# Which engine computes the rounding rest of h, of the first weight pieces and of the first half of h2

## The chip, the cores and the metric

One core of one Trainium2 chip runs the whole program. The metric is the time of one execution on the device in microseconds (us): 1650.13 us as the median of 3 runs (1648.28 to 1652.7) before the change. About 0.3% (5 us) is what a measurement of this kernel can tell from no change.

## The reference, cut to what matters

One decoder layer, batch 1, 1024 rows (positions) by 1024 columns, all in float32:

```
[shift1, scale1, gate1, shift2, scale2, gate2] = SiLU(c) W_ada + b_ada
h  = LN(x) * (1 + scale1) + shift1
one projection h W_in -> GLA q,k,v,r,gate | SWA q,k,v | branch gates
y  = sigmoid(g_A) * GLA + sigmoid(g_B) * SWA
x  = LN_1(alpha * x + gate1 * (y W_o))
h2 = LN(x) * (1 + scale2) + shift2
u  = causal conv3(h2 W_up);  f = GELU(u_gate) * u_val
x  = LN_2(alpha * x + gate2 * (f W_down))
```

The kernel multiplies with more precision than one matmul of rounded operands has: it writes each operand as a rounded part (`hi`, in the type float32r) and the rest and sums three matmuls: hi by hi, hi by lo, lo by hi. So each operand tile of 128 x 512 costs a rounding copy and a subtraction on some engine before TensorE can use it. The change is about which engine does that for three groups of tiles.

## The kernel before, in words

The order of TensorE's instructions is written by hand: the functions are called in TensorE's order, and pieces that hang on other engines (transposes, attention, layer norms) are put into a queue with `at(delay, cost, fn)` and called once a count of TensorE's expected time (`now`) has passed their due time. The other engines' instructions are ordered by the framework's planner, which works with its own costs; each engine then works through its own list in order, and an instruction that waits holds up those behind it on that engine. All loads go through SyncE's queue (SP), in order; `wst` (a weight piece as loaded, 256 KB) has 4 buffers, `aw` (a piece of W_ada) 4 in the first stage, `raw` 6 in the last.

**The head (0 to about 80 us).** x is normalised tile by tile (`norm_x`: two `bn_stats` and a `bn_aggr` on VectorE, three tiny operations on GpSimd, L361, L362 and L378, and the scaling on ScalarE, L480). The shift and scale of h come in 8 groups of 128 columns (`c` = 0 to 7): group 0 on TensorE, groups 1 to 7 as chains of 8 operations on VectorE (`mod1_part`, L525 and L527, each reading a piece `aw`), closed by a matmul with ones on TensorE (L537) and an addition on VectorE (`mods`, L538). For each group and each half of the rows `h_part` calls `to_half`: 4 transposes on TensorE (L388), the scaling into `ss` on ScalarE (L392), the rounding into `hi` on ScalarE (L397), the rest into `lo` on GpSimd (L398). TensorE multiplies it with the first weights right away (`kv_mm`, 5 PSUM banks at once, L338 to L340). These are 16 calls of `to_half`.

**The weight stream.** `ws.emit_to(n)` loads weight pieces ahead (L246), rounds on ScalarE (L253), and computes the rest (L254): on GpSimd for the first 8 pieces, which are those of the head, on VectorE for the other 100.

**Around h2 (about 900 to 1010 us).** The last output-projection units (`o_unit`, L338 to L340, evacuated on VectorE by L983) are followed per row tile by `ln_a` (layer norm with affine: statistics, GpSimd's L361 and L362, then L1068 and L1069 on VectorE) and `ln_b` (a second norm: statistics, GpSimd's three operations, L1074 on ScalarE). After row tile 3 the first half of h2 is made (`h2_part(0, kt)`, 8 calls): 4 transposes (L1085), scaling on ScalarE (L1090) into a buffer `xt` of the tag `raw`, rounding on VectorE (L1093), rest on GpSimd (L1094). After row tile 7 the second half follows (`h2_part(1, kt)`, with differences of the two halves, L1076, for a product by a Strassen-like scheme). In the same stretch the first pieces of W_up are combined on GpSimd (L1213 to L1219), the first of the 17 first products run on TensorE (L1268 to L1270), and gate2 is summed on VectorE (L602).

`split_to` (L381) is the helper that rounds on ScalarE and subtracts on VectorE; the rest of the kernel already uses it for h2's second half and for W_up and W_down.

Of the kernel before, what the change touches and what calls it, by code (L numbers as in the profile page):

```python
# [9 lines left out]
F32 = mybir.dt.float32  # L10
# [5 lines left out]
ALU = mybir.AluOpType  # L16
# [101 lines left out]
def hybrid_layer_kernel(ctx: ExitStack, tc: tile.TileContext, x, pos, wlra, wbig, wup, wdn, ada1, ada2, cst, pv, sm, lr,  # L118
                        rows, out):
    nc = tc.nc  # L120
    act, dve, pool, pe, sp = nc.scalar, nc.vector, nc.gpsimd, nc.tensor, nc.sync
# [13 lines left out]
    def ps1(name="pj"):  # L135
        return ps.tile([P, 512], F32, name=name, tag=name)
# [94 lines left out]
    class Stream:  # L231
# [8 lines left out]
        def emit_to(self, n):  # L240
            while len(self.tiles) <= min(n, len(self.items) - 1):
                src, shape, fold = self.items[len(self.tiles)]
                k, c = shape
                st = wp.tile([P, k, c], F32, name="wst", tag="wst", bufs=4)
                hi, lo = (wp.tile([P, k, c], F32R, name=n_, tag=n_) for n_ in ("whi", "wlo"))
                sp.dma_start(st, src.rearrange("p (k c) -> p k c", k=k))  # L246
                lo_eng = pool if len(self.tiles) < 8 else dve
                if fold is not None:
                    v, sl = fold
                    assert v in gate_done, v  # L250
                    dve.tensor_tensor(
                        out=st, in0=st, in1=gate[:, sl].unsqueeze(1).to_broadcast([P, k, c]), op=ALU.mult)
                act.copy(out=hi, in_=st)  # L253
                lo_eng.tensor_tensor(out=lo, in0=st, in1=hi.bitcast(F32), op=ALU.subtract)  # L254
                self.tiles.append((hi, lo))

        def get(self, n, ahead=4):
# [123 lines left out]
    def split_to(hl, src):  # L381
        act.copy(out=hl[0], in_=src)  # L382
        dve.tensor_tensor(out=hl[1], in0=src, in1=hl[0].bitcast(F32), op=ALU.subtract)  # L383

    def to_half(hT, hf, kt, xns, sc, sh, tp, tag, tp_ps, hi_dve, xb, hf32=None):

        for t in range(4):
            pe.transpose(out=tp_ps[:, t * P:(t + 1) * P], in_=xns[t][:, kt * P:(kt + 1) * P], identity=ident)  # L388
        hi, lo = hT[hf][0][:, :, kt, :], hT[hf][1][:, :, kt, :]
        if hf32 is None:  # L390
            hf32 = tp.tile([P, 4, P], F32, name=tag, tag=tag, bufs=xb)
        act.activation(out=hf32, in_=tp_ps.rearrange("p (a b) -> p a b", a=4), func=AF.Identity,  # L392
                       scale=sc[:, kt:kt + 1], bias=sh[:, kt:kt + 1])
        if hi_dve:
            dve.tensor_copy(hi, hf32)
        else:
            act.copy(out=hi, in_=hf32)  # L397
        pool.tensor_tensor(out=lo, in0=hf32, in1=hi.bitcast(F32), op=ALU.subtract)  # L398

    def split3(src, parts, eng):  # L400

# [139 lines left out]
    def h_part(c, hf):  # L541
        to_half(hT, hf, c, xn[4 * hf:4 * hf + 4], mods[:, 1], mods[:, 0], s3, "ss",
                tr_ps[:, 512 * hf:512 * hf + 512], False, 3)
# [502 lines left out]
    def t_slot(m, hl, k, dtype=F32R):  # L1046

        return hq.tile([P, 512], dtype, name=f"t{m}{hl}" + ("" if dtype == F32R else "f"), tag=f"t{m}{hl}", bufs=4)
# [3 lines left out]
    for kt in range(NK):  # L1052
        st = wp.tile([P, 512], F32, name="wst", tag="wst", bufs=4)
# [7 lines left out]
    h2 = [None, None]  # L1061
# [15 lines left out]
    rows4 = lambda v: v.rearrange("p (a b) -> p a b", a=4)  # L1077

    def h2_part(hf, kt):

        if h2[hf] is None:
            h2[hf] = [hp.tile([P, 4, NK, P], F32R, name=f"h2{hl}", tag="h") for hl in "hl"]
        pt = ps1("m")
        for t in range(4):
            pe.transpose(out=pt[:, t * P:(t + 1) * P], in_=x1[4 * hf + t][:, kt * P:(kt + 1) * P], identity=ident)  # L1085
        if hf == 0:
            f = hq.tile([P, 512], F32, name="xt", tag="raw", bufs=6)
        else:
            f = tmp["b", kt] = t_slot(3 if kt < 4 else 4, "h", kt % 4, F32)
        act.activation(out=f, in_=pt, func=AF.Identity, scale=mods[:, 3][:, kt:kt + 1], bias=mods[:, 2][:, kt:kt + 1])  # L1090
        if hf == 0:
            hi, lo = (hl[:, :, kt, :] for hl in h2[0])
            dve.tensor_copy(hi, rows4(f))  # L1093
            pool.tensor_tensor(out=lo, in0=rows4(f), in1=hi.bitcast(F32), op=ALU.subtract)  # L1094
        elif kt < 4:
            t1 = tmp["t1", kt] = t_slot(3, "l", kt, F32)
            b11 = [hl[:, :, kt, :].bitcast(F32) for hl in h2[0]]
            sub(rows4(t1), rows4(f), b11[0])
            sub(rows4(t1), rows4(t1), b11[1])
        else:  # L1100
            k = kt - 4
            t2 = tmp["t2", k] = t_slot(4, "l", k, F32)
            sub(t2, f, tmp["t1", k])
            if k % 2 == 0:
                t2h[0] = hq.tile([P, 2, 512], F32R, name="t2h", tag="t2h", bufs=2)
            tt_[2][k] = t2h[0][:, k % 2, :], t_slot(2, "l", k)
            split_to(tt_[2][k], t2)
# [44 lines left out]
    for n, t in ((2, 0), (1, 4), (2, 1), (1, 5), (2, 2), (1, 6), (2, 3), (1, 7), (2, 4), (2, 5), (2, 6), (2, 7)):  # L1152
        if n < 2:
            wo_unit(n, t)
        else:
            o_unit(t, g_o2, 512, 512, lambda: ln_tile(t))
        if n == 2 and t % 4 == 3:
            for m in range(NK):
                kt = m if t == 3 else m // 2 + 4 * (m % 2)
                at(H2_D + H2_P * m, 0.45, lambda kt=kt, t=t: h2_part(t // 4, kt))  # L1160
# [254 lines left out]
```

## Time and profile before

| | |
|---|---|
| time, median of 3 runs | 1650.13 us |
| the profiled execution's own time | 1653.21 us |
| its span, first to last instruction | 1651.5 us |
| TensorE (PE) busy | 1578.2 us, 96% |
| VectorE (DVE) busy | 1097.4 us, 66% |
| ScalarE (ACT) busy | 740.3 us, 45% |
| GpSimd (POOL) busy | 512.8 us, 31% |
| mean granted TensorE clock | 0.984 |

The shares are means over the whole span. A stretch with another limit is read by windows, by groups of lines and by waits. A time of an instruction in the timeline can overlap with the next one's start by a tenth of a microsecond.

### The profile page before, as it was taken

What the parts mean: (1) busy time and instruction counts of PE and PEld (TensorE: products, weight loads), DVE (VectorE), ACT (ScalarE), POOL (GpSimd) and SP (SyncE); (2) the same over time, 40 slices, a digit from 0 to 9 for tenths busy, and PEclk for the clock granted to TensorE, in tenths of its full rate; (3) what the DMA queues carried; (4) which work ended last, traced back from release to release, by engine and by line L of the source; (5) the groups of instructions that cost most, each with busy time, mean ns of one, the idle gap of its engine ahead of it and who ended that gap; (6) DMA issues with size and microseconds to landing.
All of it is one profiled execution on the core that took longest, in us unless ns stands there. A gap on an engine that the chain in (4) does not pass through costs nothing.

```text
span 1651.5 us, 28042 instructions
## 1 busy us (share of the span) xinstructions
PE 1578.2 (96%) x10514; PEld 1392.8 (84%) x10514; DVE 1097.4 (66%) x2110; ACT 740.3 (45%) x1700; POOL 512.8 (31%) x694
## 2 busy tenths in 40 slices
PE   5899999999999999999989779999999999999997
PEld 5899999998998998989978557778888877888886
DVE  6766666674655655535648799888888877437535
ACT  5565555554544535544522354444444444333430
POOL 5523232222542623515403732223322220003103
PEclk9999999999999999999999889999999999999999
DMA  7501010012215023010245313322222215743641
GB/s 244 170 19 42 27 27 27 27 53 80 76 52 154 27 88 104 27 53 25 71 134 160 112 51 103 108 87 77 79 81 77 77 64 191 257 138 116 204 140 51
DMA packets 79794, 152.85 MB, mean 93 GB/s; under 512 B 8981, under 2 KB 15641, under 8 KB 79658
## 3 DMA queue, kind: packets, MB, share of 16 engines
q1 hardware_dynamic: 79658, 151.07, 28.9%
q8 instruction: 82, 1.34, 0.4%
q14 instruction: 54, 0.44, 0.1%
HBM read 131.11 MB, written 19.92 MB: 91 GB/s over the span
## 4 chain that ended last, share of the span: by engine, by line
PE 78%; DVE 10%; DMA 3%; POOL 3%; ACT 2%; issue 2%; SPq 1%; POOLq 0%; DVEq 0%; ACTq 0%
PE pj L338 10%; PE pj L339 10%; PE pj L340 10%; PE w L1326 7%; PE pj L1326 4%; PE m L1326 3%; PE w L1268 3%; PE w L1270 3%; PE w L1269 3%; DVE cv L1180 2%; PE m L716 2%; PE pj L353 2%; PE m L755 2%; PE pj L354 2%; PE pj L355 2%
## 5 line engine op out<-in xcount | busy, mean ns | idle before, releaser
L338 PE MATMUL pj<-whi,hh 128*128 128x256 f32 (+1 forms) x1296 | 373.6, 288 | 0.0
L340 PE MATMUL pj<-whi,hl 128*128 128x256 f32 (+1 forms) x1296 | 367.1, 283 | 0.0
L339 PE MATMUL pj<-wlo,hh 128*128 128x256 f32 (+1 forms) x1296 | 367.0, 283 | 0.0
L338 PEld LDWEIGHTS pj<-whi,hh 128*128 128x128 f32 x1296 | 248.3, 192 | 0.6 <-issue 0.2
L339 PEld LDWEIGHTS pj<-wlo,hh 128*128 128x128 f32 x1296 | 246.8, 190 | 0.6 <-issue 0.2
L340 PEld LDWEIGHTS pj<-whi,hl 128*128 128x128 f32 x1296 | 246.5, 190 | 0.0
L382 ACT CAST whi<-wst 128x512 fp32r<-128x512 f32 x176 | 107.0, 618 | 154.9 <-PE w L1269 48.6
L383 DVE TENSOR_TENSOR wlo<-wst,whi 128x512 fp32r<-128x512 f32 x176 | 134.9, 776 | 52.6 <-ACT whi L382 52.5
L1180 DVE SCALAR_TENSOR_TENSOR cv<-u,pv_sb,cv 128x1023 f32<-128x1023 f32 x88 | 119.8, 1362 | 9.5 <-ACT cv L1178 9.4
L361 POOL TENSOR_SCALAR rs<-mv 128x1 f32<-128x1 f32 x32 | 16.1, 502 | 318.1 <-DVE mv L1339 244.9
L254 DVE TENSOR_TENSOR wlo<-wst,whi 128x512 fp32r<-128x512 f32 (+1 forms) x100 | 72.7, 745 | 40.4 <-ACT whi L253 39.2
L383 DVE TENSOR_TENSOR fl<-wst,fh 128x512 fp32r<-128x512 f32 x41 | 29.0, 708 | 82.8 <-ACT fh L382 82.8
L695 POOL TENSOR_SCALAR_AFFINE_SELECT pch<-ph 128x512 f16<-128x512 f16 x32 | 20.5, 639 | 195.8 <-ACT ph L690 195.8
L1213 POOL TENSOR_TENSOR raw<-raw 128x512 f32<-128x512 f32 x22 | 34.7, 1577 | 143.0 <-DMA raw<-in_wup 75.3
L1268 PE MATMUL pj<-h2h,whi 128*128 128x512 f32 x176 | 71.2, 405 | 5.5 <-ACT u L1275 4.2
L1219 POOL TENSOR_TENSOR wst<-wst 128x512 f32<-128x512 f32 x22 | 35.2, 1600 | 132.8 <-issue 125.3
L382 ACT CAST whi<-raw 128x512 fp32r<-128x512 f32 x66 | 40.9, 620 | 78.7 <-PE m L1269 39.2
L253 ACT CAST whi<-wst 128x512 fp32r<-128x512 f32 (+1 forms) x108 | 65.5, 620 | 19.2 <-PE pj L354 10.9
L1269 PE MATMUL pj<-h2l,whi 128*128 128x512 f32 x176 | 69.7, 396 | 0.0
L1270 PE MATMUL pj<-h2h,wlo 128*128 128x512 f32 x176 | 69.6, 395 | 0.0
L1268 PE MATMUL m<-h2h,whi 128*128 128x512 f32 x176 | 69.3, 394 | 0.0
L1269 PE MATMUL m<-h2l,whi 128*128 128x512 f32 x176 | 69.1, 393 | 0.0
(462 smaller groups left out, 4507.9 us busy)
## 6 DMA issues: line engine op xcount, KB each, us to landing
wst<-in_wbig SPq DMA_DIRECT2D x112, 256.0 KB, 3.1
wst<-in_wdn SPq DMA_DIRECT2D x88, 256.0 KB, 3.3
aw<-in_ada SPq DMA_DIRECT2D x80, 256.0 KB, 3.3
wst<-in_wup SPq DMA_DIRECT2D x52, 256.0 KB, 2.7
raw<-in_wup SPq DMA_DIRECT2D x44, 256.0 KB, 3.0
fd<-cv SPq DMA_DIRECT2D x22, 512.0 KB, 4.1
wst<-fd SPq DMA_DIRECT2D x44, 256.0 KB, 3.2
y<-in_x SPq DMA_DIRECT2D x8, 512.0 KB, 9.0
```

Of the source, the lines that this page charges most:

```text
L253: act.copy(out=hi, in_=st)
L254: lo_eng.tensor_tensor(out=lo, in0=st, in1=hi.bitcast(F32), op=ALU.subtract)
L338: pe.matmul(acc, lhsT=lh, rhs=wh, start=kt == 0 if start is None else start, stop=False)
L339: pe.matmul(acc, lhsT=lh, rhs=wl, start=False, stop=False)
L340: pe.matmul(acc, lhsT=ll, rhs=wh, start=False, stop=kt == NK - 1 if stop is None else stop)
L382: act.copy(out=hl[0], in_=src)
L383: dve.tensor_tensor(out=hl[1], in0=src, in1=hl[0].bitcast(F32), op=ALU.subtract)
L1180: dve.scalar_tensor_tensor(out=c_[:, lag:S], in0=u[:, 0:S - lag], scalar=wv[:, 2 - lag:3 - lag], in1=c_[:, lag:S], op0=ALU.mult, op1=ALU.add)
L1268: pe.matmul(acc, lhsT=wh[:, kt, :], rhs=bh, start=p not in (2, 3) and kt == 0, stop=False, **go)
L1269: pe.matmul(acc, lhsT=wh[:, kt, :], rhs=bl, start=False, stop=False, **go)
L1270: pe.matmul(acc, lhsT=wl[:, kt, :], rhs=bh, start=False, stop=kt == 3, **go)
L1326: pe.matmul(acc, lhsT=l_[:, ts_], rhs=r_, start=i == 0 and n == 0, stop=i == NFF - 1 and n == 2)
```

## The change

For three groups of tiles the subtraction moves from GpSimd to VectorE: the 16 rests of h (L398), the rests of the first 8 weight pieces (L254), and the 8 rests of h2's first half (L1094). For the last group the rounding also moves, from VectorE (L1093) to ScalarE, because `split_to` is used.

```diff
-                lo_eng = pool if len(self.tiles) < 8 else dve
...
                 act.copy(out=hi, in_=st)
-                lo_eng.tensor_tensor(out=lo, in0=st, in1=hi.bitcast(F32), op=ALU.subtract)
+                dve.tensor_tensor(out=lo, in0=st, in1=hi.bitcast(F32), op=ALU.subtract)
...
             act.copy(out=hi, in_=hf32)
-        pool.tensor_tensor(out=lo, in0=hf32, in1=hi.bitcast(F32), op=ALU.subtract)
+        dve.tensor_tensor(out=lo, in0=hf32, in1=hi.bitcast(F32), op=ALU.subtract)
...
         if hf == 0:
-            hi, lo = (hl[:, :, kt, :] for hl in h2[0])
-            dve.tensor_copy(hi, rows4(f))
-            pool.tensor_tensor(out=lo, in0=rows4(f), in1=hi.bitcast(F32), op=ALU.subtract)
+            split_to([hl[:, :, kt, :] for hl in h2[0]], rows4(f))
```

The matmuls, their order and the loads stay as they are.

## Rows read from the trace of the kernel before

**Rows 1.** The page: busy time, TensorE's tenths by slice, one group of lines.
```profile
PE 1578.2 (96%) x10514; PEld 1392.8 (84%) x10514; DVE 1097.4 (66%) x2110; ACT 740.3 (45%) x1700; POOL 512.8 (31%) x694
...
PE   5899999999999999999989779999999999999997
...
L254 DVE TENSOR_TENSOR wlo<-wst,whi 128x512 fp32r<-128x512 f32 (+1 forms) x100 | 72.7, 745 | 40.4 <-ACT whi L253 39.2
```

**Rows 2.** Windows: stretch, length, busy by engine (count), granted clock, DMA.
```profile
30.50:40.30 9.80, 6.83 (x27) 5.89 (x28) 8.44 (x10) 4.79 (x9) 8.34 (x6) 1.00 0.31 88
...
62.70:69.40 6.70, 6.65 (x42) 6.41 (x42) 6.28 (x11) 3.82 (x6) 2.84 (x2) 0.75 0.83 241
...
912.00:924.00 12.00, 9.62 (x34) 7.89 (x35) 9.62 (x14) 5.26 (x6) 11.46 (x14) 0.72 0.33 116
945.00:991.00 46.00, 37.00 (x155) 27.78 (x153) 45.09 (x66) 25.55 (x45) 13.58 (x8) 0.90 0.18 55
```

**Rows 3.** Groups of lines, 20 to 63 us, VectorE then GpSimd: count, busy, mean ns.
```profile
L527 DVE SCALAR_TENSOR_TENSOR acc<-aw,csil,acc 128x256 f32<-128x256 f32 x39 | 31.0, 795 | 1.4 <-DMA aw<-in_ada 0.2
...
L398 POOL TENSOR_TENSOR hl<-ss,hh 128x512 fp32r<-128x512 f32 x10 | 13.8, 1388 | 5.4 <-ACT hh L397 5.4
L254 POOL TENSOR_TENSOR wlo<-wst,whi 128x512 fp32r<-128x512 f32 x7 | 9.8, 1400 | 6.9 <-ACT whi L253 6.9
```

**Rows 4.** Lines 527, 254 and 1068, whole trace: duration min/median/max, first and last start.
```profile
L527 DVE SCALAR_TENSOR_TENSOR acc<-aw,csil,acc x49: 478/485/1555, 23.5 to 71.4; 128x256 f32<-128x256 f32 x49
...
L254 DVE TENSOR_TENSOR wlo<-wst,whi x100: 675/692/1225, 64.4 to 820.7; 128x512 fp32r<-128x512 f32 x96, 128x544 fp32r<-128x544 f32 x4
...
L1068 DVE SCALAR_TENSOR_TENSOR y<-y,mv,g1b x8: 1272/1284/2310, 864.4 to 931.7; 128x1024 f32<-128x1024 f32 x8
```

**Rows 5.** The chain that ended last, 0 to 90 us: start, length, what.
```profile
27.95 1.25 ACT y L480
...
29.72 0.66 PE w L537 x4
...
31.45 1.39 DVE acc L527
```

**Rows 6.** Groups of lines, 905 to 950 us, VectorE then GpSimd.
```profile
L1069 DVE SCALAR_TENSOR_TENSOR y<-y,rs,b1b 128x1024 f32<-128x1024 f32 x3 | 6.9, 2289 | 2.6 <-POOL rs L362 2.5
L1093 DVE CAST h2h<-xt 128x512 fp32r<-128x512 f32 x8 | 5.5, 698 | 1.6 <-ACT xt L1090 1.6
L1068 DVE SCALAR_TENSOR_TENSOR y<-y,mv,g1b 128x1024 f32<-128x1024 f32 x3 | 4.9, 1620 | 0.0
...
L1094 POOL TENSOR_TENSOR h2l<-xt,h2h 128x512 fp32r<-128x512 f32 x8 | 11.4, 1451 | 0.0
```

**Rows 7.** Waits, 30 to 63 us: who for whom, total, times, longest.
```profile
PE w L537 <- DVE acc L527: 4.0, 3, 2.4
PE w L338 <- DVE mods L538: 2.4, 3, 1.8
PE m L340 <- POOL hl L398: 1.5, 1, 1.5
```

**Rows 8.** VectorE's timeline, 885 to 1012 us: start, length, what.
```profile
934.75 2.28 DVE L1069 SCALAR_TENSOR_TENSOR y<-y,rs,b1b 128x1024 f32<-128x1024 f32 x1 [1.78 <-POOL rs L362]
...
950.50 0.68 DVE L1076 TENSOR_TENSOR t3lf<-t3hf,h2h 128x512 f32<-128x512 f32 x1
951.10 0.68 DVE L383 TENSOR_TENSOR t2l<-t4lf,t2h 128x512 fp32r<-128x512 f32 x1
```

**Rows 9.** The chain that ended last, 880 to 1030 us.
```profile
912.38 5.31 POOL h2l L1094 x4
917.78 0.29 POOL rs L361
```

**Rows 10.** Waits, 902 to 945 us.
```profile
PE m L1085 <- ACT xt L1090: 3.9, 1, 3.9
...
PE pj L1268 <- DVE y L983: 1.3, 1, 1.3
```

## The prediction, made before the changed kernel ran

> **What bounds the kernel now.** The page comes first: TensorE is busy 96% of the span, VectorE 66%, GpSimd 31% [rows 1]. Read no further and nothing on VectorE or GpSimd could matter. TensorE's busy tenths by slice say where that is untrue: 5 and 8 in the first two slices, 7, 7 and 9 in slices 24 to 26 [rows 1]; a slice is 41 us. All three edits lie in these two places. Their windows show the other engines: from 30.5 to 40.3 us VectorE is busy 8.44 and GpSimd 8.34 of 9.8 us while TensorE has 6.83; from 912 to 924 us VectorE has 9.62 and GpSimd 11.46 of 12 us at a granted TensorE clock of 0.72 [rows 2]. So in both places VectorE and GpSimd are full at the same time, and work moves from one to the other.
>
> Next, the groups of lines in the head. The chain of mod1 runs 39 L527 on VectorE with a mean of 795 ns [rows 3]; over the whole trace the same line has a median of 485 and a maximum of 1555 ns [rows 4]. What the long ones share is a GpSimd subtraction beside them, 1388 to 1400 ns long [rows 3]: the chain of waits has an L527 of 1.39 us [rows 5], as long as GpSimd's operation. The same holds around h2: L1068 and L1069 take 1272 ns at the least [rows 4], but L1069 has a mean of 2289 ns there and L1068 1620 [rows 6]. A large GpSimd subtraction therefore costs VectorE about 0.9 to 1.0 us whenever VectorE has a two-input operation to run. The waits say that TensorE pays for it in the head: 4.0 us for the end of the chain (L537), 2.4 us for mods, 1.5 us for GpSimd's lo itself [rows 7].
>
> **The change part by part.** The price of a subtraction on VectorE: two of them, back to back, start 0.60 us apart [rows 8], and L254 on VectorE lasts 692 ns at the median [rows 4]; I take 0.60, 0.69 as the upper end.
>
> *The head.* Between 20 and 63 us GpSimd runs 10 L398 and 7 L254 [rows 3]. Removed: 39 x (0.795 - 0.485) = 12.1 us of stretching on VectorE. Added: 17 x 0.60 = 10.2 us (11.7 at 0.69). VectorE comes out 1.9 us lighter (0.4 at the least), on a stretch where it is the engine that TensorE waits for. Then the latency: a lo is ready 0.69 instead of 1.39 us after its rounding. TensorE's 1.5 us on GpSimd's lo [rows 7] was for a lo queued behind a weight's lo; I count half, 0.7. Earlier, the norm of x ends through GpSimd: L378, then L480 at 27.95, then transposes and L537 at 29.72 [rows 5]. Two L254 and one L398, 1.39 us each, stand ahead of that in GpSimd's list and go; but the chain of group 1 on VectorE, 3 subtractions (1.8 us) longer, is late next, and I leave 0.8 us of gain. Head: 1.9 + 0.7 + 0.8 = 3.4 us. What starts ends earlier frees `aw` buffers earlier, so SP's loads, which are issued as VectorE frees them, move forward too. The 6 L398 and the pieces after 63 us cost nothing either way: TensorE is busy 6.65 of 6.7 us from 62.7 [rows 2], and if that cover went, VectorE would still pay only 0.60 for each. From there to 900 us TensorE carries whatever was gained.
>
> *h2's first half.* Removed from VectorE: 8 roundings L1093, 5.5 us [rows 6]. Added: 8 x 0.60 = 4.8 us. Removed from GpSimd: 8 L1094, 11.4 us [rows 6]. With them goes stretching of L1068 and L1069: 6.9 + 4.9 - 6 x 1.28 = 4.1 us in all [rows 4, 6]. One long L1069, at 934.75 [rows 8], lies after the last L1094 and is owed to the weight sums L1213 to L1219, which stay; I take off its 1.0. That leaves VectorE 0.7 + 3.1 = 3.8 us lighter. The chain of waits runs through GpSimd here: four L1094 in a row for 5.31 us, then L361 of the next norm [rows 9], which VectorE's L1069 and ScalarE's L1074 wait for in turn. That L361 comes forward by some 2.5 us (most of the 5.31), and what is late next is VectorE's own list. TensorE stands 3.9 us for L1090 and 1.3 us for L983 [rows 10]; the second goes, the first shrinks by about one L1094 (1.3 us). VectorE's 3.8 and TensorE's 1.3 + 1.3 with about 1.3 of clock agree, and I set this part at 4.0 us, between the bare swap of instructions (0.7) and the whole 4.1 of stretching, the 0.7 and the clock (below), 8.2.
>
> *ScalarE* gets 8 roundings, about 0.62 us each by the window's other casts (25.55 us in 45 instructions, a mean of 0.57, from 945 us [rows 2]): 5.0 us into a stretch where it is busy 5.26 of 12 us [rows 2]. Hidden, except the last one before h2's first product: 0.6 us if the cover fails. The `raw` buffer is free 0.62 + 0.69 us after the scaling instead of 0.70 + 1.45 [rows 6], so SP's loads of W_up into that tag are not held longer.
>
> A rule that speaks against all this: the Trainium skill (Perfetto Trace Analysis, Optimizing Scalar/DVE Operations) says that when VectorE is saturated, moving work to ScalarE or GpSimd may make sense; this change goes the other way on a full VectorE. By that rule alone, with nothing given back, the 10.2 us would be added. The same section adds that the two share a read port and that moving work between them might not help; the stretched rows bear out that half.
>
> **The sum.** 3.4 + 4.0 = 7.4 us. The profiled execution took 1653.21 us, 1651.5 of it the span and 1.7 around it; less 7.4 that is 1645.8. It ran 3.1 us above the median of the runs, so against 1650.13 the forecast is 1642.7 us.
>
> **The rivals.**
>
> *VectorE waits in line for ScalarE's roundings (slower).* A lo on VectorE waits for its rounding and holds up what stands behind it there, L527 and mods, for which TensorE waits; GpSimd could afford that wait, VectorE can't. The 100 L254 that are already on VectorE waited 39.2 us for L253 [rows 1], 0.39 each. For 17 in the head and 8 around h2 that is 9.8 us, so 1642.7 + 9.8 = 1652.5. It decides from a mean wait of 7.4 / 25 = 0.30 us. For it: it is what this very line does elsewhere. Against it: over the kernel VectorE has a third of its time free [rows 1], and waits there cost nothing; from 945 to 991 us, where it is full and has many such pairs, it is idle 0.9 of 46 us [rows 2].
>
> *VectorE is just overloaded (slower).* If the long L527 have another cause than GpSimd, nothing is given back: 10.2 us added in the head, 4.8 - 5.5 around h2, 9.5 in all: 1659.6. For it: VectorE at 8.44 of 9.8 us. Against it: an L527 as long as GpSimd's operation, and 485 ns elsewhere.
>
> *The head's gain is swallowed (no change).* Loads of `aw` or TensorE's own work take over after each group, and only h2's 4.0 us remain: 1646.1. Or the head's 3.4 remain and h2's gain is eaten by VectorE's full list from 945 us, 45.09 of 46 us [rows 2]: 1646.7. For it: TensorE is busy 6.65 of 6.7 us right after the head. Against it: it was idle about 3 of 9.8 us inside it [rows 2].
>
> *The clock comes back too (faster still).* From 62.7 to 69.4 us the granted clock is 0.75 and from 912 to 924 us 0.72 [rows 2], each after TensorE had stood waiting. At full clock these would give back 6.7 x 0.25 = 1.7 and 12 x 0.28 = 3.4 us: 1637.6. Against it: the 3.9 us wait only shrinks.
>
> **How the numbers follow.** The forecast, a gain of 4 to 10 us, gets 0.45; the clock 0.17; the swallowed gain 0.23; waiting in line 0.10; overload 0.05. A measurement of this kernel tells 0.3%, 5 us, from no change. Faster by more: the clock and most of the forecast, 0.55. Within it: the swallowed gain, the forecast's low end and a share of the waiting, 0.30. Slower: overload and the rest, 0.15. The range goes from 1634, the clock with the head's upper end, to 1654, the waiting in line with 1.5 us of the spread of runs; 1659.6 is left out. The forecast's own range is 1640 to 1646.
>
> **What the changed profile would show.** L527 at a mean near 0.5 us between 20 and 63 us; no L1069 above 1.3 us before the first L1213; 24 more subtractions on VectorE at about 0.69 us in the head, 8 around h2; TensorE starting its last group of the head 3 us earlier and the first L1074 of h2's second half 6 to 8 us earlier. VectorE idle before L398 or L254 for ScalarE, more than 0.3 us each, would make the prediction wrong by the first rival; an L527 that stays long with GpSimd silent, by the second.

## The result, and the profile after

The changed kernel takes 1641.91 us (median of 5 runs, 1640.19 to 1644.44) against 1650.13 us before: a ratio of 0.9946, 95% interval 0.9933 to 0.9959. Timed a second time, beside other kernels, it took 1643.86 us against 1650.23 us, ratio 0.9968 (0.9956 to 0.9980). So it is faster, by 8.2 and 6.4 us between the medians, and both intervals lie wholly below 1; 1642.7 was forecast. The profiled execution took 1640.19 us.

Where the time went is read best from marks: the first start of an operation that both kernels have. All numbers are from one profiled execution each, in us from the span's start: the end of the head is the first branch-gate tanh on ScalarE, "h2" the first transpose of x for h2, "t4" the first product with a t4 tile, "GELU 3" the third GELU.

| kernel | head end | h2 | t4 | GELU 3 | h2 to t4 | h2 to GELU 3 |
|---|---|---|---|---|---|---|
| before | 79.3 | 902.0 | 983.3 | 1027.4 | 81.3 | 125.4 |
| changed | 73.9 | 894.1 | 971.1 | 1016.0 | 77.0 | 121.9 |
| changed, again | 73.7 | 892.8 | 969.5 | 1016.3 | 76.7 | 123.5 |

The head is 5.4 us shorter and the stretch from the first transpose to t4 4.3 us; of the latter 0.8 to 2.7 us are given back until the third GELU. Between head end and h2, where the code is the same, the profiled execution of before took 822.7 us; the twelve others here took 817.8 to 821.8, mean 820.0, with the old and the new code mixed. So the 2.5 us between the first two profiles there are put down to that one execution and not to the change. The two spans differ by 13.1 us and the medians by 8.2; of the 4.9 between, these 2.5 are a part, and another 1.7 lie behind the third GELU.

The windows of the changed kernel, in the head at the times of [rows 2] (columns as there, GpSimd's the last busy time):

```profile
30.50:40.30 9.80, 6.11 (x29) 4.97 (x28) 8.38 (x20) 5.94 (x10) 0.00 (x0) 0.75 0.81 259
...
62.70:69.40 6.70, 6.30 (x54) 6.22 (x55) 5.04 (x12) 3.95 (x7) 0.53 (x1) 1.00 0.20 66
```

GpSimd is idle where it was busy 8.34 of 9.8 us, and VectorE is no fuller (8.38 after 8.44) although it does twice as many instructions there (20 for 10). The clock's low stretch has moved, from 62.7 to 69.4 us (0.75 before, 1.00 now) to 30.5 to 40.3 (1.00 before, 0.75 now). The groups of lines from 20 to 63 us say why VectorE is no fuller (each line number of the head is one less than before):

```profile
L526 DVE SCALAR_TENSOR_TENSOR acc<-aw,csil,acc 128x256 f32<-128x256 f32 x43 | 19.9, 481 | 0.7 <-DVE mv L369 0.2
L397 DVE TENSOR_TENSOR hl<-ss,hh 128x512 fp32r<-128x512 f32 x12 | 8.2, 684 | 0.9 <-ACT hh L396 0.9
L253 DVE TENSOR_TENSOR wlo<-wst,whi 128x512 fp32r<-128x512 f32 x8 | 5.4, 685 | 0.7 <-ACT whi L252 0.7
...
L524 DVE TENSOR_SCALAR acc<-aw,csil 128x256 f32<-128x256 f32 x7 | 2.4, 346 | 0.6 <-DMA aw<-in_ada 0.6
```

The mod1 operation is down from a mean of 795 ns [rows 3] to 481, the unhindered 485 of [rows 4]. The first operation of each mod1 chain, with one input (L525 before, L524 now), shrank too: from 3.8 us for 7 before, 537 ns each, to 2.4 us, 346 ns each. VectorE waits for ScalarE's roundings 0.9 + 0.7 us for 20 rests, 0.08 us each. From 14 to 84 us the waits are larger, 6.2 us for 28 rests (24 moved ones and 4 that were VectorE's before), 0.22 us each; most of that lies at the head's two ends:

```profile
DVE hl L397 <- ACT hh L396: 3.7, 5, 1.2
...
DVE wlo L253 <- ACT whi L252: 2.5, 3, 1.7
```

TensorE's waits from 30 to 63 us, beside [rows 7]: mods is gone, GpSimd's lo went from 1.5 us to 0.3 for VectorE's, and the wait for the end of the mod1 chain is as long as it was:

```profile
PE w L536 <- DVE acc L526: 4.1, 2, 3.4
PE m L339 <- DVE hl L397: 0.3, 1, 0.3
```

On the chain of waits that ended last, from 20 us to the head's end, the mod1 operation L527 has 44% before (54% in the profile of h2 alone, which has the same head) and 10% now.

Around h2, VectorE's groups from 894 to 935 us answer to [rows 6]:

```profile
L1068 DVE SCALAR_TENSOR_TENSOR y<-y,rs,b1b 128x1024 f32<-128x1024 f32 x4 | 7.2, 1795 | 2.9 <-POOL rs L361 2.9
L382 DVE TENSOR_TENSOR h2l<-xt,h2h 128x512 fp32r<-128x512 f32 x8 | 6.4, 806 | 2.3 <-ACT h2h L381 2.3
L1067 DVE SCALAR_TENSOR_TENSOR y<-y,mv,g1b 128x1024 f32<-128x1024 f32 x3 | 4.9, 1626 | 0.0
```

Here the stretching has not gone: L1067 and L1068 took 12.1 us for 7, against 7 x 1.28 = 9.0, so 3.1 of the 4.1 us are still there. VectorE's and GpSimd's timelines show what stands beside them now:

```profile
910.77 2.32 DVE L1067 SCALAR_TENSOR_TENSOR y<-y,mv,g1b 128x1024 f32<-128x1024 f32 x1
913.01 1.78 DVE L382 TENSOR_TENSOR h2l<-xt,h2h 128x512 fp32r<-128x512 f32 x1
914.71 2.32 DVE L1068 SCALAR_TENSOR_TENSOR y<-y,rs,b1b 128x1024 f32<-128x1024 f32 x1
```

```profile
910.17 1.83 POOL L1210 TENSOR_TENSOR raw<-raw 128x512 f32<-128x512 f32 x1
912.08 2.16 POOL L1211 TENSOR_TENSOR raw<-wst,raw 128x512 f32<-128x512 f32 x1
914.32 1.63 POOL L1212 TENSOR_TENSOR wst<-raw,wst 128x512 f32<-128x512 f32 x1
```

With GpSimd's list free, the weight sums of W_up (L1210 to L1216, before L1213 to L1219) begin at 910 us instead of 925, which is 16 us after the first transpose instead of 23; they stand beside the same VectorE instructions as the rests did. TensorE's waits moved too. The kernel before has one more line beside [rows 10], TensorE's wait for ScalarE's copies of u (total in us, times, longest):

```profile
PE pj L1268 <- ACT u L1275: 4.2, 2, 2.7
```

From 890 to 945 us of the changed kernel:

```profile
PE m L1084 <- ACT y L1073: 4.8, 1, 4.8
...
PE m L1084 <- ACT xt L1089: 2.6, 1, 2.6
...
PE pj L1265 <- DVE y L982: 1.5, 1, 1.5
...
PEld pj L1265 <- ACT u L1272: 0.3, 1, 0.3
```

The 3.9 us for L1090 became 2.6, the 1.3 us for L983 stayed (1.5) [rows 10], the 4.2 us for the copies of u are gone but for 0.3 of a weight load, and a new wait of 4.8 us stands before the transposes of the second half, because the first products now finish before the last norm does. Together they were 3.9 + 1.3 + 4.2 = 9.4 us and are 4.8 + 2.6 + 1.5 = 8.9. From the first transpose to the first scaling of the second half, one window of before, then of the changed kernel and of its second profile:

```profile
902.00:945.50 43.50, 34.02 (x144) 26.33 (x143) 35.24 (x47) 14.91 (x20) 34.60 (x35) 0.88 0.35 120
```

```profile
894.10:934.20 40.10, 31.19 (x143) 24.64 (x142) 33.16 (x47) 19.55 (x29) 24.02 (x26) 0.94 0.41 132
```

```profile
892.80:932.80 40.00, 30.70 (x143) 24.32 (x142) 33.23 (x47) 19.48 (x28) 23.96 (x26) 0.96 0.40 132
```

TensorE stands idle 9.5 us before and 8.9 and 9.3 us after: nearly the same. It is busy 34.0 us before and 31.2 and 30.7 us after for the same work, at a mean granted clock of 0.88 against 0.94 and 0.96. So by busy time most of the 3.4 us that this window lost look like less time at the lower of the clock's two levels (1.2 and 2.4 GHz). But that is not what set the window's end. In the kernel before, the chain that ended last leads from 902 us to the last norm's scaling on ScalarE (L1074) through no TensorE instruction: it goes through the eight L1094 (11.3 us), the weight sums and the norms. Its last part (start, length, what; asked from 880 to 1030 us):

```profile
938.28 1.34 POOL wst L1215
939.64 0.63 ACT whi L382
...
943.40 1.24 ACT y L1074
```

and VectorE's part between the last two:

```profile
940.29 1.22 DVE L383 TENSOR_TENSOR wlo<-wst,whi 128x512 fp32r<-128x512 f32 x1 [0.61 <-ACT whi L382]
941.42 0.20 DVE L370 BATCH_NORM_AGGREGATE mv<-bst 128x2 f32<-128x12 f32 x1
```

In the changed kernel no rest on GpSimd is left, and VectorE's own list is on the chain:

```profile
910.85 2.24 DVE y L1067
...
914.71 2.32 DVE y L1068
...
932.37 1.25 ACT y L1073
...
933.67 0.47 PE m L1084
```

The last norm's scaling (L1074, now L1073) begins 41.4 us after the first transpose before, and 38.3 and 38.4 us in the changed kernel's two profiles, 3.1 us earlier; the first scaling of the second half starts 1.7 to 2.1 us behind it in each. Before, the scaling ends at 944.64 us and TensorE's transposes of it begin at 944.81, so had TensorE come there sooner, it could have begun at most 0.2 us earlier; in the changed kernel it has come sooner and stands 4.8 and 3.5 us waiting for the norm. One reason why the norm comes earlier can be followed: before, its statistics (L370) stood behind the rest of a weight piece (L383) that waited for a sum on GpSimd (L1215, to 939.6 us); now all sums of this stretch are done by 926.7. The other 0.9 us of the 4.3 lie between this window and t4; what they come from was not examined.

### The profile page after: what moved, and what is told of

Its sections match the earlier page's. It is cut to its first block, busy times and chain, and to the rows that moved or that the text cites. A ratio compares the mean times of both kernels' runs of the same rounds, so it can differ in the third digit from the quotient of the medians.

```text
span 1638.4 us, 28034 instructions
## 1 busy us (share of the span) xinstructions
PE 1570.4 (96%) x10513; PEld 1386.8 (85%) x10514; DVE 1092.1 (67%) x2134; ACT 745.7 (46%) x1708; POOL 471.7 (29%) x662
## 4 chain that ended last, share of the span: by engine, by line
PE 80%; DVE 10%; issue 3%; DMA 3%; POOL 2%; ACT 2%; SPq 0%; POOLq 0%; DVEq 0%; ACTq 0%
PE pj L337 10%; PE pj L338 10%; PE pj L339 10%; PE w L1323 7%; PE pj L1323 4%; PE m L1323 3%; PE w L1265 3%; PE w L1267 3%; PE w L1266 3%; PE m L715 2%; PE pj L352 2%; PE m L1265 2%; PE m L754 2%; PE m L1266 2%; PE m L1267 2%
## 5 line engine op out<-in xcount | busy, mean ns | idle before, releaser
L360 POOL TENSOR_SCALAR rs<-mv 128x1 f32<-128x1 f32 x32 | 15.3, 478 | 327.2 <-DVE mv L1336 243.3
L253 DVE TENSOR_TENSOR wlo<-wst,whi 128x512 fp32r<-128x512 f32 (+1 forms) x108 | 78.3, 743 | 42.2 <-ACT whi L252 41.8
L1210 POOL TENSOR_TENSOR raw<-raw 128x512 f32<-128x512 f32 x22 | 35.9, 1631 | 141.3 <-DMA raw<-in_wup 75.6
L1216 POOL TENSOR_TENSOR wst<-wst 128x512 f32<-128x512 f32 x22 | 36.3, 1649 | 132.8 <-issue 125.4
L601 DVE SCALAR_TENSOR_TENSOR gate<-aw,csil,gate 128x512 f32<-128x512 f32 (+1 forms) x70 | 56.8, 823 | 18.6 <-DMA aw<-in_ada 18.2
```

The lines of the kernel that those rows point to most:

```text
L253: dve.tensor_tensor(out=lo, in0=st, in1=hi.bitcast(F32), op=ALU.subtract)
```

## The experiments

Each kernel was timed against the kernel before on the same chip; its ratio carries a 95% interval. "The changed kernel's" time is 1641.91 us in the first timing and 1643.86 in the second.

**The head alone.** Both head edits on VectorE; h2 as before.

```diff
-        pool.tensor_tensor(out=lo, in0=hf32, in1=hi.bitcast(F32), op=ALU.subtract)
+        dve.tensor_tensor(out=lo, in0=hf32, in1=hi.bitcast(F32), op=ALU.subtract)
-                lo_eng = pool if len(self.tiles) < 8 else dve
+                lo_eng = dve
```

Expected: 

> Only the head of the change: the 16 rests of h and the first 8 weight rests on VectorE, h2 as before. My theory (VectorE sheds the stretching by GpSimd): TensorE reaches the end of the head about 5.4 us earlier, as in the profile of the changed kernel, and the time is 1650.1 - 5.4 = 1644.7 us. Rival (the 2.5 us that the changed kernel also gained between 80 and 870 us come from the order of instructions that the planner changed there): about 1642.

Measured: 1645.92 us, ratio 0.9973 (0.9963 to 0.9983): 4.6 us. In its profile the head ends at 75.7 us, 3.6 us earlier. Six profiled executions with this head (this one, the changed kernel twice, and the three kernels below that leave it alone: h2's rounding on VectorE, h2's shadow, late sums) end it at 73.1 to 75.7, mean 74.3: 5.0 us. The head is the larger part, and stands by itself; its 4.6 us are a little less than the 5.4 expected.

**h2 alone.** `split_to` for h2's first half; the head as before.

Expected: 

> Only h2's first half: rounding on ScalarE, rest on VectorE; the head as before. My theory: 1650.1 - 3.6 = 1646.5 us, the first product some 2.5 us earlier than before and the stretch to 1010 us about 3.6 us shorter. Rival (the gain around h2 hangs on being early from the head or is swallowed by GpSimd's weight sums): within 1 us of 1650.1.

Measured: 1650.22 us, ratio 0.9997 (0.9987 to 1.0006): no change. Yet from the first transpose to t4 it takes 76.9 us, as in the changed kernel. Then it loses: 123.7 to the third GELU, 46.8 us from t4 on instead of 44.1 before. The order of VectorE's, ScalarE's and GpSimd's instructions there is that of the changed kernel; what differs most is the granted clock, 0.82 in that window (0.88 before, 0.92 in the changed kernel's first profile, 0.82 in its second):

```profile
975.40:1022.20 46.80, 38.50 (x138) 29.54 (x137) 43.74 (x50) 18.58 (x23) 18.80 (x10) 0.82 0.26 85
```

```profile
971.10:1016.00 44.90, 36.13 (x141) 27.57 (x141) 43.12 (x49) 18.25 (x22) 18.85 (x10) 0.92 0.27 87
```

TensorE is busy 38.5 us for work that takes 36.1 us at the better clock. So the gain around h2 is real up to t4 and partly given back behind it. The time is the one that the rival gave; up to t4 neither of its reasons holds. My number for this run, 3.6 us, was the changed kernel's first profile, the best of the series. By the medians the two parts give 4.6 + 0.3 = 4.9 us of the whole's 6.4 to 8.2; the intervals overlap, so whether the two edits gain something together is neither shown nor excluded.

**A shadow on GpSimd.** The changed kernel, with a GpSimd subtraction of equal size beside each rest of the head; nothing waits for its result.

```diff
         dve.tensor_tensor(out=lo, in0=hf32, in1=hi.bitcast(F32), op=ALU.subtract)
+        pool.tensor_tensor(out=gate[:, 0:512], in0=hi.bitcast(F32), in1=hi.bitcast(F32), op=ALU.subtract)
```

(and the same after the first 8 weight rests)

Expected: 

> The changed kernel, plus 24 subtractions on GpSimd in the head that read the rounded tile (twice) and write a tile that is overwritten later; nothing waits for their result. My theory (a GpSimd instruction that reads SBUF holds VectorE's two-input instructions up for its own length): the mod1 operations on VectorE go back from a mean of 0.48 to about 0.8 us, with VectorE also doing the rests; the time is 1641.9 + 17 x 0.7 = about 1654 us. Rival (the gain came from the shorter wait for each rest and from GpSimd's queue being empty before the norm's scalars): within 2 us of 1641.9.

Measured: 1657.84 us, ratio 1.0044 (1.0031 to 1.0058); the head ends at 88.0 us, 14 us later than without the shadow. VectorE's and GpSimd's groups from 20 to 70 us:

```profile
L529 DVE SCALAR_TENSOR_TENSOR acc<-aw,csil,acc 128x256 f32<-128x256 f32 x36 | 23.7, 674 | 0.6 <-DVE mv L371 0.2
L399 DVE TENSOR_TENSOR hl<-ss,hh 128x512 fp32r<-128x512 f32 x10 | 9.4, 936 | 0.2 <-ACT hh L398 0.2
L253 DVE TENSOR_TENSOR wlo<-wst,whi 128x512 fp32r<-128x512 f32 x9 | 7.6, 863 | 3.4 <-ACT whi L252 3.4
```

```profile
L400 POOL TENSOR_TENSOR gate<-hh 128x512 f32<-128x512 f32 x10 | 12.6, 1257 | 19.8 <-ACT hh L398 19.8
L255 POOL TENSOR_TENSOR gate<-whi 128x512 f32<-128x512 f32 x8 | 10.0, 1256 | 0.9 <-ACT whi L252 0.3
```

The time is 3.8 us above the 1654 expected. The long mod1 operations are back (674 ns, not quite the 0.8 that I expected, because a part of the holding now falls on the rests, 936 and 863 ns instead of 685). This shadow does work that nobody needs and costs more than the whole change gains.

**Fills instead of subtractions.** The changed kernel, with three GpSimd fills of each scaled tile after its last use.

```diff
         dve.tensor_tensor(out=lo, in0=hf32, in1=hi.bitcast(F32), op=ALU.subtract)
+        for _ in range(3):
+            pool.memset(hf32, 0.0)
```

Expected: 

> The changed kernel, plus three fills on GpSimd (some 0.53 us each) of each of the 16 scaled tiles of h in the head, after their last use: GpSimd is as long beside VectorE's chain as with its subtraction, but it writes SBUF and reads nothing. My theory (what holds VectorE's two-input instructions up is GpSimd's reading): the mod1 operations stay at a mean of 0.48 us, the head ends at 73 to 75 us, and the time is that of the changed kernel within 2 us. Rival (any GpSimd instruction on SBUF does it): mean 0.65 us or more, the head ends after 80 us, 1648 us or more.

Measured: 1644.88 us, ratio 0.9960 (0.9949 to 0.9971), within the changed kernel's; the head ends at 76.4 us, later than the 73 to 75 expected (perhaps because each fill also keeps its tile longer; that was not tested). From 20 to 74 us on VectorE, and from 20 to 63 us on GpSimd:

```profile
L528 DVE SCALAR_TENSOR_TENSOR acc<-aw,csil,acc 128x256 f32<-128x256 f32 x49 | 22.8, 479 | 1.6 <-DMA aw<-in_ada 0.9 <-DVE mv L369 0.2
...
L526 DVE TENSOR_SCALAR acc<-aw,csil 128x256 f32<-128x256 f32 x7 | 3.5, 498 | 0.6 <-DMA aw<-in_ada 0.4
```

```profile
L399 POOL MEMSET ss<- 128x512 f32 x33 | 17.4, 530 | 18.3 <-DVE hl L397 17.3
```

GpSimd is busy 17.4 us there and the mod1 operation keeps its 479 ns: what holds VectorE's two-input instructions up is not GpSimd's being busy or writing; what the subtraction has and the fill has not is the reading (it is also another kind of instruction, which these runs don't separate). The one-input L526 does suffer from the fills (498 ns, 346 without). The Trainium skill (SBUF — State Buffer, Who interferes with whom) names the reading: a VectorE instruction with two SBUF inputs contends with a GpSimd instruction that reads SBUF, not with one that only writes it, and one-input forms can contend in their two-port modes. The two traces agree with the first half in their 674 and 479 ns.

**Each half of the head.** Only the 8 weight rests, or only h's 16 rests, on VectorE (one of the two edits of the first experiment each).

Expected, weights: 

> Only the first 8 weight rests on VectorE, h's 16 on GpSimd as before, h2 as before. My theory (what counts in the head is each GpSimd subtraction beside VectorE's chain, and GpSimd's queue): 8 of the 24 subtractions go, a third of the head's 3.6 to 5.4 us: 1 to 2 us, about 1649 us. Rival (weights' rests hold h's rests up in GpSimd's queue, so freeing them is the whole gain): 1645 to 1646 us.

Expected, h: 

> Only h's 16 rests on VectorE, the weights' on GpSimd as before, h2 as before. My theory: two thirds of the head's gain, about 1647 us. Rival (the weights' rests are the whole gain): 1650 us.

Measured: weights alone 1649.66 us, ratio 0.9999 (0.9990 to 1.0007), head end 78.8; h alone 1648.8 us, ratio 0.9990 (0.9976 to 1.0003), head end 77.1. By head ends 0.5 and 2.2 us, together less than the 3.6 to 6.2 of both. The times tell neither from no change. Both gains were expected larger (1 to 2 and about 3 us); that the weights' rests are the whole gain is excluded by the head ends.

**h2's rounding back on VectorE.** The changed kernel with `dve.tensor_copy(hi, rows4(f))` and the rest on VectorE.

Expected: 

> The changed kernel, but h2's first half is rounded on VectorE again, as before, with the rest on VectorE too. My theory (ScalarE's roundings are hidden and relieve a full VectorE): 8 x 0.30 = 2.4 us more on VectorE, of which TensorE pays 1 to 2: 1643 to 1644 us. Rival (VectorE's wait for ScalarE's rounding costs as much as the rounding itself): 1641.9 or less.

Measured: 1645.68 us, ratio 0.9967 (0.9953 to 0.9982), runs from 1638.94 to 1648.21; h2 to t4 78.9 us, 1.9 more than with ScalarE's rounding, but 123.0 to the third GELU, no more than the changed kernel's 121.9 to 123.5. The local cost is within the 1 to 2 us expected; on the whole time it can't be told from the changed kernel.

**The changed kernel again.** Unchanged.

Expected: 

> The changed kernel once more, on the same chip as the runs beside it. If the 8.2 us are more than the 4.6 us of the head alone plus nothing of h2 alone, it gives 1642 again (within 1.5 us); if the first result was a lucky chip, 1644 to 1646. Its profile also shows whether the granted clock falls in the same places around h2 (0.79, 0.85, 0.72, 0.85, 0.71, 0.86 in 8 us slices from the first transpose) or in others.

Measured: 1643.86 us, as given above: between the two cases. Its lower clock falls elsewhere than in the first profile (0.82 from t4 to the third GELU, not 0.92). Of the seven executions with this code around h2 and GpSimd free there, six have 0.82 in that window and only the first has 0.92, so the first profile was a lucky one; whether that is also why the first median was 1.9 us lower isn't shown.

**A shadow around h2.** The changed kernel with a GpSimd subtraction after each `split_to` of h2's first half, reading the rounded part and overwriting the dead scaled tile.

```diff
             split_to([hl[:, :, kt, :] for hl in h2[0]], rows4(f))
+            hi0 = h2[0][0][:, :, kt, :].bitcast(F32)
+            pool.tensor_tensor(out=rows4(f), in0=hi0, in1=hi0, op=ALU.subtract)
```

Expected: 

> The changed kernel, plus 8 subtractions on GpSimd around h2 that read the rounded tile and overwrite the scaled tile, which nobody reads any more: GpSimd's queue and its reads are as before the change, VectorE and ScalarE do their new work too. My theory (h2's 4.3 us up to the first t4 product are VectorE's stretching and GpSimd's queue before the norm's scalars): from the first transpose to the first t4 product it takes 81 us or more again instead of 77, and the time is 3 to 6 us above the changed kernel's. Rival (the gain is the swap of a rounding for a subtraction and the earlier rest): 77 to 78 us, time unchanged.

Measured: 1646.95 us, ratio 0.9973 (0.9963 to 0.9982), just that of the head alone; h2 to t4 79.9 us: 2.9 of the 4.3 us are lost again, less than the 81 us expected. The window to the first scaling of the second half, and VectorE's groups from 895 to 945 us:

```profile
895.70:940.00 44.30, 33.66 (x143) 26.13 (x142) 32.62 (x47) 19.32 (x28) 33.24 (x35) 0.88 0.36 119
```

```profile
L1068 DVE SCALAR_TENSOR_TENSOR y<-y,rs,b1b 128x1024 f32<-128x1024 f32 x4 | 7.7, 1923 | 1.9 <-POOL rs L361 1.9
...
L1067 DVE SCALAR_TENSOR_TENSOR y<-y,mv,g1b 128x1024 f32<-128x1024 f32 x4 | 5.1, 1279 | 0.0
```

Its L1067 and L1068 are stretched by 12.8 - 8 x 1.28 = 2.6 us, less than the 3.1 in the changed kernel, and it is slower all the same. So up to the second half of h2 it isn't VectorE's stretching that counts but GpSimd's list, which is full again (33.24 of 44.3 us): the weight sums are late, VectorE stands 3.2 us waiting for ScalarE's rounding of such a piece ahead of the last norm's statistics, and that norm's scaling begins 42.7 us after the first transpose (38.3 without the shadow). TensorE's clock of before (0.88) is back as well; TensorE still waits 1.4 us for the norm.

**Weight sums later.** The changed kernel with `prep_to(n + (7 if n > 10 else 4))`.

Expected: 

> The changed kernel with GpSimd's first weight sums for W_up put into the list 3 products later (a lookahead of 4 instead of 7 products for the first 11), so that the scalars of the last norms are not queued behind them. My theory (TensorE's 4.8 us wait for the last ln_b comes through GpSimd's queue): that wait falls below 3 us, and the time is 1 to 3 us below the changed kernel's. Rival (the norm's chain on VectorE is as late, or the late sums stall the products): no change, or slower.

Measured: 1644.52 us, ratio 0.9955 (0.9938 to 0.9971): no change against the changed kernel. TensorE's wait for the last norm is 4.8 us still, and GpSimd's list has the same order: L1211 before L377, L1212 before the next L360. The planner put the sums where it had them, so the edit didn't move what it was meant to move, and what the wait is worth stays untested. Where it comes from, the changed kernel's trace tells in part: the last norm's L360 on GpSimd stands 3.7 us waiting for VectorE's statistics, so there it hangs on VectorE's list; but VectorE's L1068 ahead of them had waited 2.2 us for L361, which stood behind the sum L1212 on GpSimd.

**Group 1 on TensorE.** The changed kernel with `MOD_PE = 2`.

Expected: 

> The changed kernel with group 1 of the shift and scale computed on TensorE like group 0, so that VectorE has 6 chains of 8 operations in the head instead of 7. My theory (VectorE still sets the head's pace after the change, TensorE waits 5.5 us for L537): 3.9 us come off VectorE against some 3 us on a TensorE that is waiting for the norm of x anyway, 1 to 3 us faster than the changed kernel: 1639 to 1641 us. Rival (TensorE or the loads of W_ada are next): 1641.9 or slower.

Measured: 1643.98 us, ratio 0.9966 (0.9953 to 0.9978), no better; the head ends at 77.3 us, 3.4 us later. Of group 1's small matmuls on TensorE the profile has 19, which took 3.47 us, 0.18 each; by that the 32 take about 5.8 us (an estimate), more than the 3.2 us that came off VectorE (L526 from 22.8 to 19.9, L524 from 2.4 to 2.1). My 3 us for them was too low, and my 3.9 us for VectorE too high; the time is the rival's.

## Why the prediction was right, point by point

**The bound.** Right for the head: shadow and fills show that VectorE's two-input instructions are held up by GpSimd's subtractions and not by its being busy, and the mod1 operations left the chain that ended last (44% to 10%). The second rival (overload) is out: with GpSimd silent the operations are short.

**The head's terms.** 12.1 us of stretching was the forecast for 39 of the mod1 operations; over all 49 the line went from 38.7 to 22.8 us, 15.9 us off, for 24 rests at a pace of 0.60, 14.4 us. The prediction left out the one-input L525, which lost another 1.4 us (3.8 to 2.4), so VectorE's net relief is 2.9 us and not the 1.9 forecast. The head's sum, 3.4 us, was low: profiles give 3.6 to 6.2, mean 5.0, and the head alone is timed at 4.6. That leaves about 2.1 us for latency and GpSimd's list, for which 0.7 + 0.8 were counted; of the 1.5 us that TensorE waited for the rest, 1.2 went, not half. The runs don't take these two apart. TensorE's idle time from 20 us to the head's end doesn't size them either: it fell from 59.3 - 48.7 = 10.6 to 53.9 - 46.4 = 7.5 us, but the same old head in the profile of h2 alone has 13.7 us of it, with less busy time (45.8) and the same end.

**h2's term.** 4.0 us were forecast. Seven profiled executions with this code and GpSimd free there (the changed kernel twice, h2 alone, the shadow in the head, the fills, late sums, group 1 on TensorE) take 76.9 us on the mean from h2 to t4 (75.9 to 77.6), the four with the old code around h2 81.1 (80.8 to 81.3): 4.2 us. The path was right: before, the chain runs through GpSimd's rests and the next norms; without them the last norm comes 3.1 us earlier (L361 was forecast 2.5 us earlier), and VectorE's own list is late next, as forecast. But the working failed: "That leaves VectorE 0.7 + 3.1 = 3.8 us lighter" did not happen. The rests took 6.4 us, more than the 5.5 of the roundings, and the weight sums moved up into the place that the rests had left and stood beside L1067 and L1068 instead, so only 1.0 us of stretching went. (The sign it named came true, no L1068 above 1.3 us ahead of the first sum; the stretched ones stand beside the sums.) The prediction took the sums as fixed in time; what was freed on GpSimd was their start. Of TensorE's two waits the one for L1090 shrank by 1.3 us as forecast, the one for L983 stayed (1.3 to 1.5) and a wait for the norm came in their place. The term's 1.3 us of clock can't be shown here, since in all seven executions TensorE waits 3.5 to 4.8 us for the norm at that point. And more than half is given back: over the same executions h2 to the third GELU takes 123.8 us on the mean (121.9 to 124.7) and 125.6 (124.9 to 126.6): 1.8 us remain, less than half of the 4.0 forecast. The prediction had no term for this loss behind t4; it stands only among its rivals.

**The sum.** 5.0 + 1.8 = 6.8 us against the forecast 7.4: two errors of opposite sign, each about 2 us, so that the total came so close is luck. The profiled execution of before was 3.1 us above the median, and between head end and h2, which the change doesn't touch, 2.7 us above the others' mean; that the prediction went by the median kept this out.

**The rivals.** Waiting in line was priced at 0.39 us a rest and decides from 0.30. In the dense part of the head it was 0.08, from 14 to 84 us 0.22; around h2 it was 2.3 / 8 = 0.29, and in the profile of the head alone 7.8 us for 27 rests, 0.29 as well. So it stayed under the bound, in places only just, and what it cost in time was not measured. "The head's gain is swallowed" was wrong; its mirror, h2's gain eaten by what follows, holds by more than half, behind t4. The clock rival didn't come: in the head the mean granted clock from 20 us to its end went from 0.97 to 0.91; around h2 it rose, from 0.88 to 0.94 and 0.96 up to the second half, where TensorE then waited for the norm, and behind t4 it is 0.82 in six of seven executions, against 0.88 before.

**Open.** Which waits are followed by the lower clock differs from one execution to the next of the same code (0.92 and 0.82 in one window); no run here settles what decides it. It may also be why runs of a kernel spread over 4 to 9 us; that was not tested.

## What to carry to other kernels

Where VectorE and GpSimd are both full in one stretch, look for VectorE operations as long as GpSimd's; if two-input operations there are longer than their median elsewhere, GpSimd's work is partly paid for by VectorE, and moving it over costs VectorE little or nothing. Ask next what comes forward on the engine that was freed: here the weight sums moved into the gap and stretched the same operations, but they were also done earlier, and the norm no longer stood behind them. A shorter busy time of TensorE at a higher clock is no gain by itself if it then waits longer for something else: look which instruction the chain that ended last runs through. And an edit in a stretch where TensorE waits moves the clock as well as the wait, so judge it by several executions.

## What the runs showed of the hardware

A GpSimd subtraction that reads SBUF held VectorE's 0.48 us operations to a mean of 0.67 us (0.80 before the change), while GpSimd fills in the same place left them at 0.48; the same fills took a one-input VectorE operation from 0.35 to 0.50 us. In these runs the two engines' conflict depends on what GpSimd's instruction does, not on both being busy at once.
